# Operand halves loaded in place, ten gate tiles, and a reordered second projection in a hybrid decoder block

## The chip, the core and the metric

The kernel runs on one core of a Trainium2 chip. Its engines are TensorE (PE in the profile, with PEld for its weight loads), VectorE (DVE), ScalarE (ACT), GpSimd (POOL) and SyncE (SP, which issues nearly all transfers here). Each runs its own instructions in order and waits for the others by semaphores. The metric is device time in microseconds; smaller is better.

## The reference

One decoder block, batch 1, 1024 tokens of width 1024, all float32. Cut to the part in question:

```python
o_r = retention(qr, kr, vr)                         # 4 heads, chunks of 128 tokens, a running state
o_r = (head_groupnorm(o_r, ret_gn_g[l], ret_gn_b[l]) * jax.nn.silu(gr)).astype(x.dtype)
y = jax.nn.sigmoid(gate_a) * (o_a @ w_proj_a[l]) + jax.nn.sigmoid(gate_b) * (o_r @ w_proj_b[l])
x = x + y @ w_out[l]
```

Before it come an RMS norm, one input projection and dilated attention (whose result is o_a, 512 wide); behind it a squared-ReLU MLP.

## The kernel before

**Numbers in two halves.** A float32 operand x is used as a pair: xh, x rounded to the type that TensorE multiplies, and xl = x - xh. `split` (L349) makes the pair, xh on ACT (L350) and xl on DVE (L353). A product takes three matmuls a term: high by high, high by low, low by high. A group of 4 terms is 12 matmuls of 128x512.

**Stages around the change.** (1) *Retention*: 4 heads by 8 chunks of 128 tokens. For each chunk `values` multiplies the input by the head's value weights, and beside it run `decay`, `output`, `update` and, a chunk later, `turn_o`. `output` ends in a chain: ACT copies the result out of PSUM into `on` (L994), DVE takes its mean and variance (L996, L997, L998), POOL a power (L999), DVE scales (L1000, L1001). `turn_o` transposes `on` on TensorE (L1026, into `tr`), ACT scales it (L1031), and sums of it are stored to `on_d`, the operands of the second projection. (2) *First projection*: 16 groups (8 blocks of 128 outputs by 2 halves of the tokens), `oa` times w_proj_a; each result is multiplied with its gate (L1103 sigmoid on ACT, L1104 product on DVE) and stored to `pa_d`. (3) *Second projection*, tag "pb": 8 units j of 7 Strassen products, N1 to N7, each of one weight piece (A holds N1 and N2, B N6 and N3, C N5 and N7, D N4) with one operand of `on_d`. Units 0 to 3 take the first token half's operands, 4 to 7 the second's. `product` (L400) runs one and copies it out of PSUM (`ms` L419, `u` L424 and L427); `result` combines, gates and stores or, from unit 4 on, splits into the operands of (4) by `keep`. (4) *Output projection*, `w_out`.

**Where operands lie.** XS holds the block's input in three slots, (0,0), (1,0), (1,1), and a fourth, (0,1), while the retention needs them; ES are four slots that come free when the retention's tiles do. A slot is a pair xh, xl of 128 x 4 x 512. Before the change, `oa` (4 parts, `load_oa`) and the second projection's first operands are loaded into staging tiles of a pool of three (`pr`, name `oraw`, 512 KB each, `load_sum`) and split from there (`part_sum`); the later ones into tiles `s` of 256 KB (`load_part`), two splits for each 512 KB. The gates for (2) are loaded into a pool of four tiles (`pm2`) and, while ES[3] is unused, into its eight half rows (`places`, `spare`); a gate that lies there is written by its sigmoid into a tile of `pm2`.

**What sets the order.** TensorE's order is written out (L299, `manual_schedule`). A scheduler orders the other engines by its own estimate of times, but for instructions that `keep_in_program_order` pins to the place where the program calls them. Weights come by `Weights`: raw tiles are loaded in order as their places come free, and a list of steps splits them (and forms sums of them for B and C, `sums`). With `pace` 1 each `tick`, one a product, runs at most one step, no sooner than `lag` ticks behind the load of its raw tile. In the second projection `lag` is 2.

## Time and profile before

| | |
|---|---|
| median of 3 runs | 2179.03 us (2178.85 to 2179.24) |
| the profiled execution | 2176.74 us, its span 2175.0 us |
| TensorE idle in the span | 2175.0 - 2151.6 = 23.4 us |

By stretch, with the busy time of each engine (PE, PEld, DVE, ACT, POOL, each with the number of its instructions), the granted clock as a share of full speed, the DMA engines' busy share and GB/s:

```profile
1180.00:1285.00 105.00, 104.50 (x494) 85.64 (x493) 75.21 (x145) 59.13 (x116) 27.89 (x33) 1.00 0.56 168
1285.00:1320.00 35.00, 32.18 (x140) 25.67 (x138) 27.80 (x36) 22.15 (x31) 0.00 (x0) 1.00 0.93 318
1320.00:1400.00 80.00, 79.47 (x348) 64.90 (x347) 59.04 (x83) 41.49 (x68) 0.00 (x0) 1.00 0.77 263
1400.00:1470.00 70.00, 66.80 (x291) 54.03 (x290) 58.78 (x85) 35.60 (x54) 0.00 (x0) 1.00 0.75 243
```

The last head's end and the first projection lie in the first two rows, the second projection in 1300 to 1464. In a row of the timeline the first number is the start, the second the length; a bracket gives the idle time of that engine just before and what ended it. A row of a DMA is its issue; when it landed is another view.

### The profile page before, as it was taken

Reading aid. Unit: us, or ns where it says so; the run is one execution under the profiler, and the core shown is the slowest. Engines: PE = TensorE matmul, PEld = TensorE weight load, DVE = VectorE, ACT = ScalarE, POOL = GpSimd, SP = SyncE. Lnnn points to the kernel's source line nnn. Section 1 sums busy time; section 2 is a strip of 40 time slices with the busy share of each in tenths; the row PEclk is TensorE's granted clock in tenths of the full one; section 3 lists DMA queues with packets and bytes.
Section 4 is the critical chain, followed back from the end, with each engine's and each line's share of the span. In section 5 each row is a group of like instructions: output and inputs, shape, how many; then the busy total and the mean of one; then the engine's idle time right before and its main releaser. Section 6 shows DMA issues by size and latency. Waiting matters only on the chain. (4 is left out here: it accounts for less than half of the span.)

```text
span 2175.0 us, 28668 instructions
## 1 busy us (share of the span) xinstructions
PE 2151.6 (99%) x9928; PEld 1764.2 (81%) x9928; DVE 1356.0 (62%) x2327; ACT 1098.4 (51%) x2097; POOL 316.0 (15%) x340
## 2 busy tenths in 40 slices
PE   9999999999999999999999999999999999999999
PEld 6887777788888888888888877778788888888887
DVE  5723443565556665657776767783865556788884
ACT  5425555444655554545555655552654545755552
POOL 1000000000000000002123120000000000777773
PEclk9999999999999999999999999999999999999999
DMA  6323333333658676664364487774255556745443
GB/s 210 133 82 93 109 104 102 100 130 120 202 170 241 199 222 191 199 200 140 110 193 121 128 288 268 259 239 154 88 150 160 151 146 204 235 152 191 166 140 107
DMA packets 294579, 358.81 MB, mean 165 GB/s; under 512 B 35025, under 2 KB 202385, under 8 KB 294178
## 3 DMA queue, kind: packets, MB, share of 16 engines
q1 hardware_dynamic: 293890, 356.72, 52.4%
q8 instruction: 78, 1.28, 0.2%
q14 instruction: 67, 0.55, 0.1%
q10 hardware_dynamic: 544, 0.26, 0.0%
HBM read 240.33 MB, written 116.59 MB: 164 GB/s over the span
## 5 line engine op out<-in xcount | busy, mean ns | idle before, releaser
L353 DVE TENSOR_TENSOR wl<-raw,wh 128x1024 fp32r<-128x1024 f32 (+1 forms) x308 | 343.0, 1115 | 462.6 <-ACT wh L350 461.5
L350 ACT ACTIVATE wh<-raw 128x1024 fp32r<-128x1024 f32 (+1 forms) x308 | 296.0, 963 | 297.9 <-PE ms L247 106.6
L247 PE MATMUL mm<-xh,wh 128*128 128x512 f32 x960 | 387.7, 404 | 2.3 <-ACT ms L419 2.2
L247 PE MATMUL mm<-xl,wh 128*128 128x512 f32 x960 | 374.2, 390 | 0.9 <-DVE xl L353 0.9
L247 PE MATMUL mm<-xh,wl 128*128 128x512 f32 x960 | 375.0, 391 | 0.0
L247 PE MATMUL ms<-xh,wh 128*128 128x512 f32 x784 | 318.0, 406 | 4.5 <-ACT u L427 2.9
L247 PE MATMUL ms<-xh,wl 128*128 128x512 f32 x784 | 306.2, 391 | 1.4 <-DVE wl L353 1.4
L247 PE MATMUL ms<-xl,wh 128*128 128x512 f32 x784 | 305.6, 390 | 0.0
L247 PEld LDWEIGHTS mm<-xh,wl 128*128 128x128 f32 x960 | 180.2, 188 | 39.6 <-DVE wl L353 0.7
L247 PEld LDWEIGHTS mm<-xh,wh 128*128 128x128 f32 x960 | 180.5, 188 | 37.4 <-ACT ms L419 3.0
L247 PEld LDWEIGHTS mm<-xl,wh 128*128 128x128 f32 x960 | 180.7, 188 | 35.3 <-DVE xl L353 1.3
L247 PE MATMUL mm<-wh,xh 128*128 128x512 f32 x458 | 186.1, 406 | 0.1
L247 PEld LDWEIGHTS ms<-xh,wh 128*128 128x128 f32 x784 | 147.4, 188 | 45.2 <-issue 10.1
L999 POOL TENSOR_TENSOR st<-st,half 128x1 f32<-128x1 f32 x32 | 25.8, 807 | 1075.6 <-DVE st L998 1075.6
L247 PE MATMUL mm<-wh,xl 128*128 128x512 f32 x458 | 179.6, 392 | 0.9 <-DVE xl L353 0.9
L247 PE MATMUL mm<-wl,xh 128*128 128x512 f32 x458 | 178.5, 390 | 0.0
L247 PEld LDWEIGHTS ms<-xh,wl 128*128 128x128 f32 x784 | 147.1, 188 | 33.7 <-DVE wl L353 1.8
L247 PEld LDWEIGHTS ms<-xl,wh 128*128 128x128 f32 x784 | 147.6, 188 | 26.9
L247 PEld LDWEIGHTS mm<-wh,xl 128*128 128x128 f32 x458 | 86.0, 188 | 20.6 <-DVE xl L353 1.4
L247 PEld LDWEIGHTS mm<-wh,xh 128*128 128x128 f32 x458 | 86.2, 188 | 16.1 <-ACT xh L350 0.6
L247 PEld LDWEIGHTS mm<-wl,xh 128*128 128x128 f32 x458 | 86.5, 189 | 15.7
L247 PE MATMUL ms<-wh,xh 128*128 128x512 f32 x232 | 92.3, 398 | 0.0
(309 smaller groups left out, 3827.9 us busy)
## 6 DMA issues: line engine op xcount, KB each, us to landing
raw<-in_w_up SPq DMA_DIRECT2D x32, 512.0 KB, 3.8
h_d<-s SPq DMA_DIRECT2D x64, 256.0 KB, 4.3
raw<-in_w_down SPq DMA_DIRECT2D x32, 512.0 KB, 3.5
raw<-in_w_aqk_q SPq DMA_DIRECT2D x24, 512.0 KB, 3.5
qk_d<-sg SPq DMA_DIRECT2D x48, 256.0 KB, 3.0
qk<-qk_d SPq DMA_DIRECT2D x24, 512.0 KB, 5.8
rb<-rs_d SPq DMA_DIRECT2D x24, 512.0 KB, 7.1
xh<-h_d SPq DMA_DIRECT2D x11, 896.0 KB, 4.6
```

The lines of the kernel that those rows point to most:

```text
L247: self.nc.tensor.matmul(ps, x, y, start=start, stop=stop, skip_group_check=not first)
L350: hi = nc.scalar.activation(dst_h, src, AF.Copy)
L353: nc.vector.tensor_tensor(dst_l, src, dst_h.bitcast(F), op=OP.subtract)
L999: nc.gpsimd.tensor_tensor(st[:, 9:10], st[:, 8:9], half[:, 0:1], op=OP.pow)
```

## The change

**In-place landing.** `load_oa`, and `load_half` for all the second projection's operands, load 512 KB straight into the low half xl of the slot that they are for. The split then reads xl: ACT writes xh from xl, DVE writes xl from xl and xh (`split_halves`, pinned on ACT). The pool `pr`, `load_sum`, `part_sum` and `load_part` go. A load is issued a product at a time, its split follows three products later. Such a load has to wait until TensorE has read what lay in that half: `oa` comes into XS(0,0) and XS(1,0), which `values` reads up to chunk 3 of the last head, N5 and N7 into XS(0,1) and XS(1,1), which it reads up to chunk 7.

**Ten gate tiles.** `pm2` has ten tiles for four, `places` and `spare` go, a sigmoid is always in place, and up to two gates a step are loaded while fewer than eight are ahead.

**Second projection.** From unit 2 on the high part of each weight split is pinned, and the four sums are two steps of two instead of riding on D's step; `lag` is 3; the tick comes after the product's results and not before.

**Its end.** `keep` of the second token half of units 6 and 7, and the whole last result (that of N3 of unit 7), are put off until all products are issued (`last`); the result before it (N4 of unit 7) is pinned on DVE, with its split, and the splits of the first four blocks of `w_out` are pinned.

On TensorE and POOL the order of instructions is the same before and after. On ACT, DVE and SP it differs, at four places as follows.

*ACT, chunks 2 and 3 of the last head* (xh<-oraw, now xh<-xl, is a part of `oa`). Before:

```order
L350 ACTIVATE xh<-oraw 128x1024
L1031 ACTIVATE onE<-tr,gng 128x128 x4
L350 ACTIVATE xh<-oraw 128x1024
L350 ACTIVATE qh<-rqT 128x256
L994 ACTIVATE on<-ms 128x512
L350 ACTIVATE Sh<-St 128x512
L350 ACTIVATE xh<-oraw 128x1024
```

Now:

```order
L1044 ACTIVATE onE<-tr,gng 128x128 x4
L356 ACTIVATE xh<-xl 128x1024
L1007 ACTIVATE on<-ms 128x512
L356 ACTIVATE qh<-rqT 128x256
L356 ACTIVATE xh<-xl 128x1024
L356 ACTIVATE Sh<-St 128x512 x2
```

The split of a part of `oa` stands ahead of `on` in both, now directly ahead of it; and its transfer can now only leave when TensorE has read the low half. On DVE its xl stands ahead of BN_STATS in both.

*DVE, chunk 6 of the last head* (xl<-oraw,xh, now xl<-xl,xh, is a half of N5). Before:

```order
L353 TENSOR_TENSOR xl<-oraw,xh 128x1024
L996 BN_STATS st<-on 128x6
L1013 SCALAR_TENSOR_TENSOR St<-St,ms 128x512
L997 BN_AGGR st<-st 128x2
L1013 SCALAR_TENSOR_TENSOR St<-St,ms 128x512
L998 TENSOR_SCALAR st<-st,rc 128x1
L353 TENSOR_TENSOR Sl<-St,Sh 128x512
L1000 TENSOR_SCALAR st<-st,rc 128x1
L968 TENSOR_TENSOR sm<-ms,maskT 128x128
L1001 TENSOR_SCALAR on<-on,st 128x512
```

Now:

```order
L359 TENSOR_TENSOR xl<-xl,xh 128x1024
L1009 BN_STATS st<-on 128x6
L1026 SCALAR_TENSOR_TENSOR St<-St,ms 128x512
L1010 BN_AGGR st<-st 128x2
L1026 SCALAR_TENSOR_TENSOR St<-St,ms 128x512
L1011 TENSOR_SCALAR st<-st,rc 128x1
L359 TENSOR_TENSOR xl<-xl,xh 128x1024
L1013 TENSOR_SCALAR st<-st,rc 128x1
L359 TENSOR_TENSOR Sl<-St,Sh 128x512
L1014 TENSOR_SCALAR on<-on,st 128x512
L359 TENSOR_TENSOR Sl<-St,Sh 128x512
```

The split of N5's first half stands ahead of the chain from BN_STATS to `on` (L1001, now L1014) in both; that of its second half and one of the state's splits (Sl) now stand inside the chain.

*ACT in unit 1 to 3 of the second projection.* Before, with u the copies out of PSUM and wh the weight splits:

```order
L419 ACTIVATE ms<-mm 128x512
L350 ACTIVATE wh_11986<-raw_11915 128x1024
L909 ACTIVATE s<-s 128x512
L350 ACTIVATE wh_11961<-raw_11524 128x1024
L427 ACTIVATE u_11944<-ms 128x512
L909 ACTIVATE s<-s 128x512
```

Now:

```order
L427 ACTIVATE ms<-mm 128x512
L356 ACTIVATE wh_11919<-raw_11512 128x1024
L435 ACTIVATE u_11914<-ms 128x512
L910 ACTIVATE s<-s 128x512
L356 ACTIVATE wh_11944<-raw_11870 128x1024
L910 ACTIVATE s<-s 128x512
```

The copy `u` of L427 (now L435) stood behind two splits of 128x1024, and now stands behind one.

*DVE at the end of the second projection* (mm and u are the last products, wl are `w_out`'s splits, xl<-s,xh the operands of the output projection). Before:

```order
L1176 TENSOR_TENSOR s<-s,ms 128x512
L353 TENSOR_TENSOR wl_13092<-raw_12998,wh_13091 128x1024
L1177 TENSOR_TENSOR s<-s 128x512
L433 TENSOR_TENSOR u_12949<-mm,u_12949 128x512
L1178 TENSOR_TENSOR s<-s 128x512
L1180 TENSOR_TENSOR s<-s,u_12949 128x512
L353 TENSOR_TENSOR wl_13103<-raw_13043,wh_13102 128x1024
L353 TENSOR_TENSOR xl<-s,xh 128x512
L1181 TENSOR_TENSOR s<-s 128x512
L353 TENSOR_TENSOR xl<-s,xh 128x512
```

Now:

```order
L1181 TENSOR_TENSOR s<-s,ms 128x512
L1188 TENSOR_TENSOR s<-s 128x512
L1181 TENSOR_TENSOR s<-s 128x512
L359 TENSOR_TENSOR wl_12974<-raw_12883,wh_12973 128x1024
L1181 TENSOR_TENSOR s<-s 128x512
L441 TENSOR_TENSOR u_12847<-mm,u_12847 128x512
L359 TENSOR_TENSOR wl_12993<-raw_12927,wh_12992 128x1024
L359 TENSOR_TENSOR xl<-s,xh 128x512 x3
L1187 TENSOR_TENSOR s<-s,u_12847 128x512
L1188 TENSOR_TENSOR s<-s 128x512
L359 TENSOR_TENSOR xl<-s,xh 128x512
```

The three operations of one result (before L1176 to L1178, now L1181 three times) now all stand ahead of the last u, and of the last result's operations (before L1180 and L1181, now L1187 and L1188) those that stood ahead of the first xl now stand behind it.

The diff, cut to its core:

```diff
@@ -111,16 +111,18 @@
-                self.split(h, l, self.raw[r][:, cols], key[0] == "up" and key[1] < 2 and key[2] != "A")
+                late = key[0] == "pb" and key[1] > 1
+                self.split(h, l, self.raw[r][:, cols], late or key[0] == "up" and key[1] < 2 and key[2] != "A")
...
-        def sums(r):
+        def sums(r, which=(0, 1, 2, 3)):
             (x22, x21), (x11, x12) = ((self.raw[i][:, 0:512], self.raw[i][:, 512:1024]) for i in (r, r - 1))
-            for x, y in ((x22, x21), (x21, x11), (x11, x22), (x12, x11)):
+            for k in which:
+                x, y = ((x22, x21), (x21, x11), (x11, x22), (x12, x11))[k]
@@ -131,7 +133,10 @@
-                piece((tag, j, "D"), (self.D, j % 2), r, slice(0, 512), lambda r=r: sums(r))
+                fine = tag == "pb" and j > 1
+                piece((tag, j, "D"), (self.D, j % 2), r, slice(0, 512), None if fine else lambda r=r: sums(r))
+                if fine:
+                    self.steps += [(set(), r, lambda r=r, k=k: sums(r, k)) for k in ((0, 1), (2, 3))]
@@ -346,11 +352,13 @@
-    def split(dst_h, dst_l, src, pin=False):
+    def split(dst_h, dst_l, src, pin=False, both=False):
...
-        nc.vector.tensor_tensor(dst_l, src, dst_h.bitcast(F), op=OP.subtract)
+        lo = nc.vector.tensor_tensor(dst_l, src, dst_h.bitcast(F), op=OP.subtract)
+        if both:
+            tc.keep_in_program_order(lo)
@@ -898,19 +906,24 @@
-    def load_sum(from_, c, name, h):
-        raw = from_.tile([P, 2, 512], F, name="oraw")
-        o = 2 * SUMS.index(name)
-        nc.sync.dma_start(raw, on_d[2 * c + h, o:o + 2].rearrange("k p t -> p k t"))
-        return raw
...
-    def part_sum(to, raw, h):
-        split(*(x[:, 2 * h:2 * h + 2] for x in to), raw, True)
+    OPB = [{"N5": XS[0, 1], "N7": XS[1, 1]}, {}]
+    begun = []
+    def load_half(at, c, name, h):
+        xh, xl = (x[:, 2 * h:2 * h + 2] for x in OPB[c][name])
+        o = 2 * SUMS.index(name)
+        nc.sync.dma_start(xl.bitcast(F), on_d[2 * c + h, o:o + 2].rearrange("k p t -> p k t"))
+        begun.append((at, xh, xl))
+    def split_halves(upto):
+        while begun and begun[0][0] <= upto:
+            _, xh, xl = begun.pop(0)
+            split(xh, xl, xl.bitcast(F), True)
@@ -941,7 +954,7 @@
-            raw = pr.tile([P, S], F, name="oraw")
+            raw = oaS[s][1].bitcast(F)
@@ -1057,8 +1070,7 @@
-                    pr = pool(load, "pr", 3)
-                    pm2 = pool(load, "pm2", 4)
+                    pm2 = pool(load, "pm2", 10)
@@ -1072,35 +1084,28 @@
-                    raws = [(name, g, load_sum(pr, 0, name, g), -3) for name, g in (("N5", 0), ("N5", 1), ("N7", 0))]
+                    for name, g in (("N5", 0), ("N5", 1), ("N7", 0)):
+                        load_half(-3, 0, name, g)
...
-        OPB = [{"N5": XS[0, 1], "N7": XS[1, 1]}, {}]
         waiting = [("N7", 1)] + [(name, h) for name in ("N1", "N2", "N4", "N6") for h in range(2)]
-        spare = []
...
-            if len(gates) == n + 3 and n + 3 < len(work):
-                e, es = work[n + 3]
+            while len(gates) < min(n + 8, len(work)):
+                e, es = work[len(gates)]
                 gates.append(loaded(pm2, sg_d[0, e, :, es], "s0"))
-            for _ in range(2 if len(gates) < n + 8 else 0):
-                if spare:
-                    e, es = work[len(gates)]
-                    gates.append(spare.pop(0))
-                    nc.sync.dma_start(gates[-1], sg_d[0, e, :, es])
+                if len(gates) > n + 5:
+                    break
...
-                s0 = gates[n + 1]
-                if s0 in places:
-                    gates[n + 1] = pm2.tile([P, 512], F, name="s0")
-                tc.keep_in_program_order(nc.scalar.activation(gates[n + 1], s0, AF.Sigmoid))
+                sigmoid(gates[n + 1])
@@ -1109,19 +1114,12 @@
-                places = [x[:, k].bitcast(F) for x in ES[3] for k in range(4)]
-                spare = list(places)
...
-            if raws and raws[0][0] in OPB[0] and raws[0][3] <= n - 2:
-                name, h, raw, _ = raws.pop(0)
-                part_sum(OPB[0][name], raw, h)
-            if waiting and waiting[0][0] in OPB[0] and (n % 2 or n > 11) and len(raws) < 3:
-                name, h = waiting.pop(0)
-                raws.append((name, h, load_sum(pr, 0, name, h), n))
-        for name, h, raw, _ in raws:
-            part_sum(OPB[0][name], raw, h)
+            split_halves(n - 3)
+            if waiting and waiting[0][0] in OPB[0] and (n % 2 or n > 11):
+                load_half(n, 0, *waiting.pop(0))
@@ -1153,10 +1151,12 @@
-        def keep(j, f, cs, y):
+        last, done = [], []
+        def keep(j, f, cs, y, pin=False):
...
-            split(yh, yl, y)
+            split(yh, yl, y, pin, pin)
@@ -1171,16 +1171,25 @@
+            if n == len(results) - 1 and n in ahead and not done:
+                done.append(n)
+                last.append(lambda: result(j, f, cs, src))
+                return
...
-                nc.vector.tensor_tensor(y, y, src, op=OP.add)
-                nc.vector.tensor_tensor(y, y, sgb, op=OP.mult)
-                nc.vector.tensor_tensor(y, y, pa[0], op=OP.add)
+                for with_, op in ((src, OP.add), (sgb, OP.mult), (pa[0], OP.add)):
+                    ins = nc.vector.tensor_tensor(y, y, with_, op=op)
+                    if n == len(results) - 2:
+                        tc.keep_in_program_order(ins)
+                if n == len(results) - 2:
+                    return keep(j, f, cs, y, True)
...
+            elif j > 5 and cs.start and n < len(results) - 1:
+                last.append(lambda: keep(j, f, cs, y))
@@ -1189,26 +1198,21 @@
-        todo, unit = [(c, name, k) for c, name in ((0, "N3"),) for k in range(4)], {}
-        begun = []
-        def load_part(c, name, k):
-            return loaded(pm3, on_d[2 * c + k // 2, 2 * SUMS.index(name) + k % 2], "s")
+        todo, unit, base = [(0, "N3", h) for h in range(2)], {}, len(work)
+        W.lag = 3
...
-            todo += [(1, after[j, name], k) for k in range(4) if (j, name) in after]
+            pipe.tick()
+            todo += [(1, after[j, name], h) for h in range(2) if (j, name) in after]
             if (j, name) == (1, "N6"):
-                todo += [(1, "N1", k) for k in range(4)]
-            while begun and begun[0][0] <= i - 3:
-                _, c, op, k, raw = begun.pop(0)
-                split(*(x[:, k] for x in OPB[c][op]), raw)
-            while todo and len(begun) < 6 and (len(begun) < 2 or begun[-2][0] < i):
-                begun.append((i, *todo[0], load_part(*todo.pop(0))))
+                todo += [(1, "N1", h) for h in range(2)]
+            split_halves(base + i - 3)
+            if todo:
+                load_half(base + i, *todo.pop(0))
@@ -1219,6 +1223,8 @@
+        for fn in last:
+            fn()
```

13 lines of the change are left out of this document (7 added, 6 removed).

## The prediction

> **What bounds the kernel now.** I read the page's busy times first, then the waits of TensorE in the stretch that the change touches (1180 to 1480 us: the last retention head, the first projection, the second, the start of the output projection), then the timeline around each wait.
>
> ```profile
> PE 2151.6 (99%) x9928; PEld 1764.2 (81%) x9928; DVE 1356.0 (62%) x2327; ACT 1098.4 (51%) x2097; POOL 316.0 (15%) x340
> ```
>
> TensorE is busy 2151.6 of 2175.0 us, and the change leaves its instructions and their order alone. Only its waits can go or come. Those of 1180 to 1480 us, by who was waited for (total, times, longest):
>
> ```profile
> PE ms L247 <- DVE s L1104: 1.5, 2, 1.2
> PE ms L247 <- DVE wl L353: 1.4, 1, 1.4
> PE mm L247 <- ACT ms L419: 1.4, 1, 1.4
> PE ms L247 <- ACT u L427: 1.1, 2, 0.7
> PE mm L247 <- DVE xl L353: 0.9, 1, 0.9
> PE ms L247 <- ACT on L994: 0.3, 1, 0.3
> ```
>
> The first five are 6.3 us in seven waits. A matmul behind a wait lasts 0.50 us (1287.08 below) where its neighbours last 0.39 (1198.35 below), so I put each wait 0.13 us above its idle time: about 7.2 us, 0.33% of the span, is all that can be won there. The sixth lies in the retention, where the change adds waits of its own.
>
> **What the change can win, part by part.** *Ten gate tiles.* The wait for L1104 is a gate's product behind a late sigmoid:
>
> ```profile
> 1285.68 0.63 ACT L1103 ACTIVATE s<-xh 128x512 f32<-128x512 f32 x1 [2.69 <-DMA pa_d<-s]
> ...
> 1287.08 0.50 PE L247 MATMUL ms<-xh,wh 128*128 128x512 f32 x1 [1.23 <-DVE s L1104]
> ```
>
> ACT sat 2.69 us because, with four tiles, the next comes free only when a store to pa_d has landed. With ten, the first ten gates load during the retention, and the eleventh needs only the first's store. The idle 1.5 with two restarts is 1.7 us; I take all of it, and 1.0 as the low end, should one late store remain.
>
> *N6's halves.* The first N2 of the second projection waits for L419, which stands on ACT behind both splits of N6:
>
> ```profile
> 1306.69 1.06 ACT L350 ACTIVATE xh<-oraw 128x1024 fp32r<-128x1024 f32 x1 [0.25 <-DMA oraw<-on_d]
> 1307.66 0.58 ACT L419 ACTIVATE ms<-mm 128x512 f32<-128x512 f32 x1
> ...
> 1308.29 0.50 PE L247 MATMUL mm<-xh,wh 128*128 128x512 f32 x1 [1.35 <-ACT ms L419]
> ```
>
> The second split waited for its transfer. The two loads went out together; now the first stands one store earlier on SP and the second has its way alone. The least that this gives is the 0.25 of the row, the most the whole wait, 1.5; I take 1.2, since both splits can then run as soon as ACT is free.
>
> *Finer steps, lag 3, pinned splits.* An evacuation of u stands on ACT behind a weight split that waits for its transfer:
>
> ```profile
> 1324.99 1.06 ACT L350 ACTIVATE wh<-raw 128x1024 fp32r<-128x1024 f32 x1 [4.89 <-DMA raw<-in_w_pb_q]
> ```
>
> ACT stood still 4.89 us with u queued behind. Pinned and a product later, this split comes behind u in the order of ACT (third excerpt above). Both such waits, 1.1 and two restarts, are 1.4; I take all of it, 0.7 as the low end. For unit 7 the sums of the raw weights now stand in one run on DVE, and its split follows at once:
>
> ```profile
> 1436.45 0.69 DVE L124 TENSOR_TENSOR raw<-raw 128x512 f32<-128x512 f32 x1
> ...
> 1439.40 2.36 DVE L353 TENSOR_TENSOR wl<-raw,wh 128x1024 fp32r<-128x1024 f32 x2
> ...
> 1440.67 0.50 PE L247 MATMUL ms<-xh,wl 128*128 128x512 f32 x1 [1.42 <-DVE wl L353]
> ```
>
> From the last sum's end to that split lie 2.26 us of other DVE work, now behind it; but lag 3 lets the sums begin a product later, behind splits of their own. Of the 1.55 I take 0.9 (0 to 1.55).
>
> *The end.* The output projection's first tile waits for a split at the end of a DVE queue:
>
> ```profile
> 1464.28 1.23 DVE L353 TENSOR_TENSOR wl<-raw,wh 128x1024 fp32r<-128x1024 f32 x1
> 1465.41 0.69 DVE L353 TENSOR_TENSOR xl<-s,xh 128x512 fp32r<-128x512 f32 x1
> ...
> 1466.16 0.50 PE L247 MATMUL mm<-wh,xl 128*128 128x512 f32 x1 [0.94 <-DVE xl L353]
> ```
>
> Of what stands on DVE between the last product's u and this split, two operations of the kind of 0.69 us leave (last excerpt above; the row of 1465.41 has that length): up to 1.4 us against a wait of 0.94, so I take 1.0 (0 to 1.05). The results put off are first read by the output projection's last tiles of the same half; 24 matmuls of 0.23 us a tile cover them, and without that cover they would cost their 0.69 each.
>
> Gains: 1.7 + 1.2 + 1.4 + 0.9 + 1.0 = 6.2 us; the ends add to 2.0 and 7.2. The larger splits cost nothing: one of 1.22 on DVE for two of 0.69, on engines that are busy 62% and 51%.
>
> **What the change adds: loads that wait for TensorE.** A staged load could start whenever staging was free. One that lands in the operand's half waits for TensorE's last read of what lay there. Its split is pinned ahead of `on` on ACT (first excerpt above), so the price is set by L, the time from issue to landing of 512 KB. The retention's rows of 1100 to 1260 us, then those of the staged tile in the whole stretch:
>
> ```profile
> oraw<-on_d SPq DMA_DIRECT2D x6, 512.0 KB, 4.0
> ```
>
> ```profile
> L350 ACT ACTIVATE xh<-oraw x16: 1040/1053/1069, 1198.7 to 1306.7; 128x1024 fp32r<-128x1024 f32 x16
> L353 DVE TENSOR_TENSOR xl<-oraw,xh x16: 1217/1223/1810, 1199.8 to 1308.1; 128x1024 fp32r<-128x1024 f32 x16
> ...
> DMA to landing us min/median/max: 3.7/5.0/6.0
> ```
>
> Place 1, chunks 3 and 4 of the last head. What matters is the chain `on`, BN_STATS, ..., `on` (L1001), transpose:
>
> ```profile
> 1198.35 0.39 PE L247 MATMUL mm<-wh,xl 128*128 128x512 f32 x1
> ...
> 1203.62 0.69 DVE L996 BATCH_NORM_STATS2 st<-on 128x6 f32<-128x512 f32 x1
> ...
> 1207.03 0.55 DVE L1001 TENSOR_SCALAR on<-on,st 128x512 f32<-128x512 f32 x1
> 1207.05 0.40 PE L247 MATMUL mm<-wh,xl 128*128 128x512 f32 x1
> 1208.67 0.60 PE L1026 MATMUL tr<-ident,on 128*128 128x128 f32 x4
> 1209.57 1.28 ACT L909 ACT_TABLE_LOAD   x1
> ...
> 1213.87 0.69 DVE L996 BATCH_NORM_STATS2 st<-on 128x6 f32<-128x512 f32 x1
> 1217.76 0.54 DVE L1001 TENSOR_SCALAR on<-on,st 128x512 f32<-128x512 f32 x1
> 1218.77 0.60 PE L1026 MATMUL tr<-ident,on 128*128 128x128 f32 x4
> ```
>
> The first oa load leaves at 1198.74, when that read ends. Its xl split stands ahead of BN_STATS on DVE; from BN_STATS to the end of L1001 are 3.96 us. With 0.2 for hand-overs `on` is ready at 1198.74 + L + 1.05 + 1.22 + 3.96 + 0.2 = 1205.2 + L, and the transposes want it at 1208.67: a wait of L - 3.5. The last oa load leaves at 1207.45; behind its xh come the table load 1.28, a sigmoid 0.63, `on` 0.60, then 4.43 to the end of L1001: 1215.7 + L against 1218.77, L - 3.0. A first wait moves the second need along with it, so both together cost the larger: L - 3.0.
>
> Place 2, chunk 6, with N5's two halves:
>
> ```profile
> 1238.72 0.39 PE L247 MATMUL mm<-wh,xl 128*128 128x512 f32 x1
> ...
> 1244.93 0.68 DVE L996 BATCH_NORM_STATS2 st<-on 128x6 f32<-128x512 f32 x1
> ...
> 1248.14 0.45 SPq L905 DMA_DIRECT2D oraw<-on_d  x1
> 1248.42 0.54 DVE L1001 TENSOR_SCALAR on<-on,st 128x512 f32<-128x512 f32 x1
> ```
>
> The load leaves at 1239.11; BN_STATS starts at 1239.11 + L + 1.05 + 1.22 + 0.2 = 1241.6 + L. To L1001's end it is 4.03 now, and 0.85 more with the second xl of N5 and a split of the state now in between (second excerpt; 1.91, of which POOL's power hides about 1.05). That is 1246.5 + L against 1248.96 now, where there is no slack left (the transposes follow at once): L - 2.5.
>
> Place 3, N7's first half:
>
> ```profile
> 1253.54 0.60 ACT L994 ACTIVATE on<-ms 128x512 f32<-128x512 f32 x1
> 1254.20 0.50 PE L247 MATMUL ms<-vh,kzh 128*128 128x512 f32 x1 [0.32 <-ACT on L994]
> ```
>
> Its load still leaves at about 1248.14, behind three stores on SP. On ACT now follow xh 1.05, smh 0.3, four onT 1.5, `on` 0.60: it ends at 1251.8 + L, and TensorE, by then L - 2.5 later, wants it at 1251.3 + L: 0.5, of which 0.3 is there already. One gate product of 0.69 now stands between BN_STATS and the state's update, ahead of which it stood: 0.9 in all.
>
> New waits: (L - 3.0) + (L - 2.5) + 0.9 = 2L - 4.6, but not under 0. The rows' ends, 3.7 and 6.0, give 2.8 and 7.4; if the hand-overs and orders hide more than I see, 0. I take L = 4.0, the median of the six loads of this size in this stretch: 3.4 us.
>
> Two statements of the Trainium skill bear on L. "DMA: Bandwidth & Descriptors", on the anatomy of one DMA (the gpsimd path, whereas these go out from SP), fits a fixed 2.0 us plus the bytes over 436 GB/s, an estimate of 3.2 us for 512 KB; the measured 3.7 at least is slower, and by the page the new waits would be 1.8 and the time 1.6 us shorter than mine. "Perfetto Trace Analysis", DMA Optimizations, speaks against two per request: smaller transfers may let some work start sooner. In this trace 256 KB of the same data take 4.8 us (first row below) and 512 KB 5.0, so by the trace splitting would win back 0.2 of L, 0.4 us of the sum.
>
> ```profile
> s<-on_d SPq DMA_DIRECT2D x32, 256.0 KB, 4.8
> oraw<-on_d SPq DMA_DIRECT2D x12, 512.0 KB, 5.0
> ```
>
> **Sum.** 3.4 - 6.2 = -2.8 us. The profiled execution's 2176.74 (2175.0 and 1.7 around it) becomes 2173.9; the median shown, 2179.03, lies 2.3 above it, so the forecast is 2176.2 us.
>
> **Rivals.** *B: the new waits don't come.* For it: DMA is quiet in the retention, and two late loads may hide behind one another. Then the gains stand alone: 2179.0 - 6.2 = 2172.8, at most 2171.8. Against it: the orders put xh ahead of `on` in three chunks, and place 2 has no slack.
>
> *C: late landings make it slower.* One mechanism: in-place loads in the retention holding ACT, and behind it `on`. From L = 5.4 the new waits exceed 6.2 and the kernel is slower than before; at 6.0 with the gains at their low end of 2.0 it is 2179.0 + 7.4 - 2.0 = 2184.4. For it: a median of 5.0 and a maximum of 6.0 over the whole stretch; SP runs in order, so each load that waits for TensorE also holds the `sr`, `rqT` and weight loads behind it, which the formula leaves out. Against it: 4.0 in this part.
>
> *D: the gains only move.* DVE stays as full at the second projection's end as it was, ACT is held by another split; with gains of 3 and the new waits of 3.4: 2179.4. Against it: the orders show the late splits moved.
>
> **How the numbers follow.** Forecast 0.43, B 0.25, C 0.22, D 0.10. This kernel's measurement tells about 0.2% from no change: 2174.7 to 2183.4. Of the forecast's own spread (2173 to 2180, from L of 3.7 to 5.0 and the gains around 6) a third lies under 2174.7; B is faster; of C four fifths are slower, the rest within; D is within. Faster 0.15 + 0.25 = 0.40, slower 0.18, same 0.42. The range of 8 in 10 reaches from B's 2171.5 to C's 2183.5.
>
> **What would show it.** Right: no waits for a gate's product around 1285; L1001 and `on` late in chunks 3, 4 and 6 of the last head, with TensorE waiting at `tr` for some 1 us and 1.5 us; ACT idle before xh<-xl, ended by its DMA; waits for wl and xl at the second projection's end under 1 us. Wrong: no wait at `tr` there (B), or an issue-to-landing of xl<-oa_d and xl<-on_d above 5.4 (C), or a wait for u or ms as long as now (D).

## The result and the profile after

The changed kernel took 2185.11 us (median of 7 executions, 2183.78 to 2188.96) against 2178.85 of the kernel before, run between them (7, 2177.48 to 2180.46): ratio 1.0030, 95% interval 1.0020 to 1.0039. It is slower by 6.3 us; the forecast was 2176.2, and the range ended at 2183.5.

The profiled execution after has a span of 2187.2 us, 12.2 more than before. 3.3 of them lie ahead of the stretch that the change touches, 2.4 of these in the attention part (550 to 900 us). In the other profiled kernels that part ahead is between 0.6 us shorter and 4.2 us longer than before, so I don't put the 3.3 down to the change. In the stretch itself, 1180 to 1480 us, are 9.0, from the start of one matmul to the start of another, the same two in both. The profiled execution is the slowest of the seven, 3.9 us above their median. Busy times on the page after:

```profile
PE 2157.8 (99%) x9928; PEld 1769.3 (81%) x9928; DVE 1353.3 (62%) x2311; ACT 1094.9 (50%) x2081; POOL 315.0 (14%) x340
```

TensorE has the same 9928 matmuls and is busy 6.2 us longer: it doesn't only wait more, its work lasts longer too. The table of busy time by stretch (start:end, length, PE, PEld, DVE, ACT, POOL, then the granted TensorE clock, the DMA share and GB/s) shows where. Before:

```profile
1250.00:1300.00 50.00, 48.17 (x212) 38.34 (x211) 32.91 (x48) 26.05 (x44) 11.99 (x14) 1.00 0.87 290
1300.00:1350.00 50.00, 48.24 (x212) 39.26 (x211) 39.09 (x53) 28.65 (x43) 0.00 (x0) 1.00 0.79 263
1400.00:1450.00 50.00, 47.88 (x210) 38.98 (x209) 43.63 (x64) 27.00 (x42) 0.00 (x0) 1.00 0.80 268
```

After:

```profile
1250.00:1300.00 50.00, 46.82 (x203) 37.42 (x203) 32.00 (x53) 25.16 (x44) 14.39 (x17) 0.97 0.76 238
1300.00:1350.00 50.00, 47.82 (x204) 38.99 (x203) 34.48 (x44) 23.14 (x31) 0.00 (x0) 0.97 0.80 268
1400.00:1450.00 50.00, 46.67 (x193) 37.67 (x193) 42.69 (x60) 25.20 (x38) 0.00 (x0) 0.93 0.72 243
```

In 1400 to 1450 us 193 matmuls are done where 210 were, at a clock of 0.93 where it was 1.00. The waits of TensorE after, in 1180 to 1480 us (total, times, longest):

```profile
PE mm L252 <- ACT xh L356: 2.7, 1, 2.7
PE tr L1039 <- DVE on L1014: 2.5, 3, 1.1
PE mm L252 <- ACT ms L427: 2.2, 1, 2.2
PE ms L252 <- ACT on L1007: 1.3, 1, 1.3
PE ms L252 <- DVE s L1109: 0.8, 1, 0.8
PE mm L252 <- DVE xl L359: 0.7, 1, 0.7
PE ms L252 <- DVE wl L359: 0.5, 1, 0.5
```

With one of 0.2 for wh that is 10.9 us, where the six lines before add to 6.6. The old waits for a gate's product around 1285, both for u and that for xl at the end are gone, and unit 7's for wl is smaller. Three places are new or worse.

**The retention.** ACT's rows in chunks 3 and 4 of the last head, then TensorE's at the two transposes:

```profile
1205.71 1.06 ACT L356 ACTIVATE xh<-xl 128x1024 fp32r<-128x1024 f32 x1 [1.74 <-DMA xl<-oa_d]
1209.47 1.06 ACT L356 ACTIVATE xh<-xl 128x1024 fp32r<-128x1024 f32 x1 [1.91 <-DMA xl<-oa_d]
...
1213.01 0.66 PE L1039 MATMUL tr<-ident,on 128*128 128x128 f32 x4 [0.92 <-DVE on L1014]
...
1223.86 0.66 PE L1039 MATMUL tr<-ident,on 128*128 128x128 f32 x4 [0.52 <-DVE on L1014]
```

In chunk 3 it is not `on` itself that the second part holds. The state's high half Sh stands behind it on ACT, and DVE, inside the chain from BN_STATS to `on`, waits for Sh:

```profile
1211.08 0.69 DVE L359 TENSOR_TENSOR Sl<-St,Sh 128x512 fp32r<-128x512 f32 x1 [1.08 <-ACT Sh L356]
```

Chunks 6 and 7, ACT's splits of N5's first half and of N7's first:

```profile
1247.92 1.06 ACT L356 ACTIVATE xh<-xl 128x1024 fp32r<-128x1024 f32 x1 [0.55 <-DMA xl<-on_d]
...
1258.05 1.06 ACT L356 ACTIVATE xh<-xl 128x1024 fp32r<-128x1024 f32 x1 [2.56 <-DMA xl<-on_d]
```

```profile
1255.21 0.63 PE L1039 MATMUL tr<-ident,on 128*128 128x128 f32 x4 [1.10 <-DVE on L1014]
...
1261.23 0.50 PE L252 MATMUL ms<-vh,kzh 128*128 128x512 f32 x1 [1.25 <-ACT on L1007]
...
1263.01 0.50 PE L252 MATMUL ms<-xh,wh 128*128 128x512 f32 x1 [0.82 <-DVE s L1109]
```

ACT stands still until a half has landed, and TensorE waits for `on`, whose chain stands behind that half or has such splits in it. These are the prediction's places 1 to 3. In chunk 6 most of the wait is the chain's length: from the start of BN_STATS to the end of L1014 it takes 4.91 us, where it took 4.03, with the xl of N5's second half and one Sl now in it.

**The first N2 of the second projection.** Its wait grew from 1.35 to 2.18 us. ACT:

```profile
1315.08 1.06 ACT L356 ACTIVATE xh<-xl 128x1024 fp32r<-128x1024 f32 x1 [0.36 <-DMA xl<-on_d]
1316.05 1.06 ACT L427 ACTIVATE ms<-mm 128x512 f32<-128x512 f32 x2
```

The evacuation `ms` still stands behind N6's second split. By the semaphores in the trace that half left at 1307.62, just behind a half of N3 that is read later, and landed 7.4 us after its issue. Ahead of it ACT had stood still 2.40 us for N4's second half, whose split is pinned ahead of N6's. Transfers are slow in this stretch: from 1285 to 1320 us the DMA engines are busy 0.98 of the time, and its ten halves took 4.6 to 8.3 us (the view's last number is of the one load whose landing it tells):

```profile
xl<-on_d SPq DMA_DIRECT2D x10, 512.0 KB, 6.7
```

**Product 38,** the last product of the second operands' N3. Its half of N3 had landed at 1411.0, but its split stands on ACT behind the split of a result, which waited 4.87 us for DVE. ACT, then TensorE:

```profile
1417.98 0.63 ACT L356 ACTIVATE xh<-s 128x512 fp32r<-128x512 f32 x1 [4.87 <-DVE s L1181]
...
1419.47 1.04 ACT L356 ACTIVATE xh<-xl 128x1024 fp32r<-128x1024 f32 x1
```

```profile
1420.56 0.80 PE L252 MATMUL mm<-xh,wh 128*128 128x512 f32 x1 [2.68 <-ACT xh L356]
```

**Half rate behind the waits.** TensorE's rows around the N2 wait (start, duration):

```profile
1316.68 0.50 PE L252 MATMUL mm<-xh,wh 128*128 128x512 f32 x1 [2.18 <-ACT ms L427]
...
1318.26 0.63 PE L252 MATMUL mm<-xh,wh 128*128 128x512 f32 x1
```

From 1318.26 to 1321.25 seven matmuls start 0.43 us apart, elsewhere 0.227. The profile's record of the granted clock says half from 1318.06 to 1321.47, which begins 1.4 us after the wait's end. It happens three times, behind 1261 to 1263 (7 matmuls), behind 1316 (7) and behind 1420 (11): 25 x 0.20 = 5.0 us. The first two of these stretches, each with the one just ahead of it (the first number behind the length is PE's busy time, the third from the end the clock):

```profile
1260.03:1263.44 3.41, 1.39 (x5) 0.87 (x6) 3.41 (x8) 1.15 (x3) 1.51 (x3) 1.00 0.31 74
1263.45:1266.86 3.41, 3.41 (x10) 2.64 (x9) 2.43 (x7) 1.26 (x2) 1.83 (x3) 0.50 0.48 136
1314.65:1318.05 3.40, 1.37 (x6) 1.15 (x7) 3.40 (x5) 3.04 (x5) 0.00 (x0) 1.00 1.04 404
1318.06:1321.47 3.41, 3.41 (x10) 2.64 (x9) 3.38 (x4) 0.40 (x2) 0.00 (x0) 0.50 1.03 357
```

The third runs from 1420.46 to 1427.28, twice as long. The three begin 54.61 and 102.40 us apart, 16 and 30 times 3.413. In the 3.41 us ahead of them TensorE was idle 2.02, 2.04 and 2.58 us.

The Trainium skill describes this: "TensorE: Matmul & The Clock Gate", Part 1 (the HAM clock gate), has half clock after an idle window of some 3.4 us that runs freely, and its table on kernels asks for no idle gap above about 3 us. The 3.41 us of half rate and the spacing by whole multiples of it agree. The limit does not: here windows in which TensorE was idle for 2.0 of 3.4 us were enough, from one wait of 2.18 us, or from 1.25 and 0.82 close together.

### The profile page after: what moved, and what is told of

It reads as the page before. It is cut to its first block, busy times and chain, and to the rows that moved or that the text cites. A ratio compares the mean times of both kernels' runs of the same rounds, so it can differ in the third digit from the quotient of the medians.

```text
span 2187.2 us, 28561 instructions
## 1 busy us (share of the span) xinstructions
PE 2157.8 (99%) x9928; PEld 1769.3 (81%) x9928; DVE 1353.3 (62%) x2311; ACT 1094.9 (50%) x2081; POOL 315.0 (14%) x340
## 4 chain that ended last, share of the span: by engine, by line
PE 87%; DVE 5%; DMA 3%; ACT 2%; issue 2%; POOL 1%; SPq 0%; POOLq 0%; ACTq 0%; DVEq 0%
PE mm L252 44%; PE ms L252 37%; PE tr L671 1%; PE tr L692 1%; DVE xl L359 1%; DMA xl<-on_d 1%; ACT wh L356 1%; PE tr L682 1%; ACT xh L356 1%; PE tr L1039 1%; PE tr L824 1%; DVE raw L126 1%; PE ms L979 0%; DVE wl L359 0%; DMA raw<-in_w_rqk_q 0%
```

## The experiments

Waits below are TensorE's in 1180 to 1480 us of each kernel's profiled execution; "slow matmuls" are those at half rate there. The clock differs between executions of one kernel, so a profile and a median need not agree within 3 us. The kernel before ran beside each group of runs, with medians of 2177.7 to 2179.0 us; the ratios are to these.

| kernel | median us | ratio to before | waits us | slow matmuls |
|---|---|---|---|---|
| before | | | 6.6 | 0 |
| after | 2185.11 | 1.0030 [1.0020, 1.0039] | 10.9 | 25 |
| oa, N5, N7 staged again | 2186.57 | 1.0036 [1.0022, 1.0050] | 11.1 | 28 |
| N6 asked for earlier | 2186.66 | 1.0038 [1.0023, 1.0053] | 12.0 | 14 |
| N3's halves paired | 2181.76 | 1.0020 [1.0011, 1.0030] | 8.6 | 0 |
| third edit undone | 2184.22 | 1.0032 [1.0023, 1.0041] | 9.4 | 7 |
| late splits | 2180.48 | 1.0011 [1.0002, 1.0020] | 6.2 | 5 |
| late splits, pairs | 2174.92 | 0.9985 [0.9976, 0.9993] | 5.8 | 5 |
| and N6 earlier | 2177.14 | 0.9992 [0.9983, 1.0001] | 5.5 | 7 |
| before, end reordered alone | 2176.64 | 0.9986 [0.9978, 0.9995] | 5.2 | 0 |
| late splits, pairs, N6 ahead of N4 | 2177.26 | 0.9997 [0.9988, 1.0005] | 4.4 | 0 |
| same, finer sums for units 2 to 5 | 2174.86 | 0.9991 [0.9983, 1.0000] | 4.9 | 6 |
| same, old steps | 2173.77 | 0.9982 [0.9973, 0.9991] | 4.2 | 0 |
| same, old steps, all pins | 2174.52 | 0.9984 [0.9975, 0.9993] | 4.7 | 0 |
| same, old steps, pins of units 3 to 6 | 2170.43 | 0.9964 [0.9950, 0.9977] | 0.0 | 0 |

**The landing in the retention: staged again.**

```diff
-                    pm2 = pool(load, "pm2", 10)
+                    pr = pool(load, "pr", 2)
+                    pm2 = pool(load, "pm2", 6)
...
-            raw = oaS[s][1].bitcast(F)
+            raw = pr.tile([P, S], F, name="oraw")
```

> Edit of the changed kernel: oa and the first three halves (N5 twice, N7 once) are staged again, in a pool of two tiles, and the gates have six tiles. Theory A (the in-place loads of the retention make `on` late): the waits of TensorE for `tr` and `on` in the last head, 1.09, 0.69, 1.26, 1.41 and 0.99 us in the changed kernel, go back to under 0.6 us each, and the stretch of doubled matmul spacing behind them at 1263 to 1267 us (1.7 us lost) goes too: 5 to 7 us less than the changed kernel, 2178 to 2180 us. Rival B (they only move to the next wait): the two long waits of the second projection grow by as much, 2183 to 2186 us.

The waits in chunks 3, 4 and 6 went (0.3 lost is left at 1250), but that behind chunk 7 grew to 2.5 us, and the time is that of the changed kernel. With two staging tiles the third load (N7's first half) left at 1249.87, where with the three tiles of the kernel before it had left at 1211.91; in the changed kernel it waits for TensorE, here for a tile. So this run did not tell landing from place.

**N6 earlier, N3 paired.**

```diff
-            if waiting and waiting[0][0] in OPB[0] and (n % 2 or n > 11):
+            if waiting and waiting[0][0] in OPB[0] and (n % 2 or n > 9):
```

> Edit of the changed kernel: from the tenth group of the first projection on, not the twelfth, one operand half is loaded a step, so N6's second half leaves a step (2.7 us) earlier. Theory C (the wait of 2.2 us at the second projection's start is N6's late landing): that wait falls under 0.5 us, and the doubled spacing of the 8 matmuls behind it (1.6 us) goes: 3 to 4 us less, 2181 to 2182 us. Rival D (the DMA engines are full there, an earlier issue lands no earlier): the wait stays at 1.5 to 2.5 us and the time at 2184 to 2186 us.

The wait at the first N2 is 1.8 us and its drop of the clock stays: asking earlier in a stretch where the DMA share is 0.96 (1285 to 1320 us) brings little.

```diff
-            if todo:
-                load_half(base + i, *todo.pop(0))
+            for _ in range(2 if i > 28 else 1):
+                if todo:
+                    load_half(base + i, *todo.pop(0))
```

> Edit of the changed kernel: N3's and N4's halves of the second token half may leave two a product. Theory E (the wait of 2.7 us and its followers of 0.65 and 0.2 at unit 4's N3 come from a split queued on ACT behind a split of a result that DVE delivers late; a load one product earlier puts it ahead): the waits for ACT xh and DVE xl around 1420 us go, and with them the doubled spacing of 16 matmuls: 6 to 8 us less, 2177 to 2179 us. Rival F (DVE is simply full there): a wait of 2 us or more stays, for another tile, 2183 to 2186 us.

Product 38 now waits 0.8 us (for wl) instead of 2.7 and 0.7, no matmul is slow, and the median is 3.4 us lower (2.2 by the ratios, whose intervals overlap; in the profiles the stretch is 6.8 us shorter). Both splits of that N3 now run at 1409.5, ahead of the result's split that waits 4.86 us for DVE. In the kernel before the quarters came at the same rate, two a product, but their splits were not pinned; a pinned one stands where the program calls it, and the call came behind that result's.

**How long a wait halves the clock.** The kernel before with six waits of growing length in the up projection:

```diff
+            if name == "N5" and j in HOLD:
+                x = maskT[:, 0, :]
+                nc.vector.tensor_copy(x, unit[j]["d"][:, :P])
+                for _ in range(HOLD[j]):
+                    nc.gpsimd.tensor_tensor(x, x, maskT[:, 1, :], op=OP.add)
+                pt = tr.tile([P, 4, P], F, name="tr")
+                nc.tensor.transpose(pt[:, 0, :], x, ident)
```

> The kernel before with six waits of TensorE of rising length built into the MLP's first products (a copy on DVE, 1, 3, 4, 5, 6 and 8 operations on GpSimd, then a transpose that nothing reads), some 38 us apart. Theory G (a wait beyond some 2.3 us makes the matmuls behind it run at half the rate for some us): spacing stays at 0.227 us behind the short waits, and is about 0.43 us for 8 to 20 matmuls behind the waits over some 2.3 us, with the granted clock under 1.00 there. Rival H (the low clock is a state of the chip in those runs and no result of waits): the spacing is 0.227 us behind all six, and the time grows by the sum of the waits alone, some 14 us.

The waits lost 2.5, 3.0, 3.5, 4.1, 5.7 and 6.7 us, start to start. Behind the first two no matmul was slow, behind the others 6 to 9 each. Read alone this is a threshold between 3.0 and 3.5 us, and the 2.2 us of the changed kernel contradict it. Hence twelve waits of nearly one length (`HOLD = {j: 2 + j % 2 for j in range(2, 14)}`):

> The kernel before with twelve waits of TensorE put into the up projection, one per unit, made as before by a chain of POOL operations that a transpose waits for: three operations (about 3.0 us of wait) at odd units and two (about 2.7) at even ones. Matmuls at half rate behind a wait tell whether the clock dropped. If a fixed length of the wait decides (between 3.0 and 3.5 us, as the six waits before would have it), all twelve behave alike within each kind, and none drops. If the share of idle time in a window of the clock's own decides, then where the wait falls in that window matters: some of the twelve drop and others of the same length don't.

The 3.41 us ahead of and behind one boundary, for two of them (PE's busy time first, clock third from the end):

```profile
1615.79:1619.20 3.41, 1.47 (x7) 1.26 (x8) 1.04 (x3) 0.87 (x1) 1.28 (x2) 1.00 0.98 302
1619.21:1622.61 3.40, 3.40 (x10) 2.63 (x9) 1.23 (x1) 0.66 (x2) 0.00 (x0) 0.50 0.45 133
1639.68:1643.09 3.41, 1.50 (x7) 1.28 (x8) 0.67 (x2) 1.06 (x1) 1.70 (x3) 1.00 1.05 333
1643.10:1646.50 3.40, 3.40 (x16) 2.80 (x16) 1.04 (x1) 0.58 (x1) 0.00 (x0) 1.00 0.27 82
```

Seven waits cost 3.0 us and five 2.5. Ten of the twelve halved the clock, six of 3.0 us and four of 2.5; one of 3.0 and one of 2.5 did not. So the length alone does not decide. What decides can be read from the record of the clock. The ten stretches of half rate begin 7 or 13 times 3.413 us apart. Cut the run into windows of 3.413 us on that grid: TensorE was idle for 1.94 to 2.84 us in the window ahead of each of the ten. A boundary divided the other two waits, and their fuller windows had 1.91 and 1.89 us. Ten of the kept traces have such stretches. Over their windows at full clock, but for the first 30 us, 1.81 us is the least that drew one and 1.91 the most that did not, so the limit lies near 1.9 of 3.41 us. The first boundary lies anywhere from 0.4 to 3.0 us behind the start of these spans, whose first instructions are the same, so the program does not set the grid, and whether a wait of 2 to 3 us draws half rate is luck.

**Is it the landing, or the place of the split?** The in-place loads stay, their splits go to where the data are there:

```diff
-                if h == RH - 1 and c >= 4:
-                    load_oa(c - 4)
+                if h == RH - 1 and c == 4:
+                    sigmoid(gates[0])
+                    for s in range(SLOTS):
+                        load_oa(s)
+                for s in {5: (0, 1), 6: (2, 3)}.get(c, ()) if h == RH - 1 else ():
+                    split(*oaS[s], oaS[s][1].bitcast(F), True)
...
-                    for name, g in (("N5", 0), ("N5", 1), ("N7", 0)):
-                        load_half(-3, 0, name, g)
+                    for at, name, g in ((0, "N5", 0), (1, "N5", 1), (2, "N7", 0)):
+                        load_half(at, 0, name, g)
```

> The changed kernel with the retention's in-place loads kept at their places (oa's four now all asked for in chunk 4, N5's halves and N7's first half in the last chunk as before), but their splits put off to where their data have surely landed: oa's at the ends of chunks 5 and 6, N5's and N7's behind the gate products 3 to 5. Theory A (the waits that are new in the retention come from the place of the pinned splits on ACT and DVE, ahead of `on`): the waits of TensorE at the transposes behind chunks 3, 4 and 6 (1.1 + 0.7, 1.3, 1.4 + 1.0 us) sink under 0.5 us together or to what the kernel before has there (about 0.5), and so does the clock's drop behind the last of them (about 1.7 us): 5 to 6 us less than the changed kernel, about 2179.5. Theory L (it is the landing itself: the transfers wait for TensorE's last read and hold SP's queue): the waits stay within 1 us of the changed kernel's, and the time at 2184 to 2186. The waits in the second projection (2.3 and 2.8 us with their clock drops) are untouched in both.

Its waits in 1180 to 1480 us:

```profile
PE mm L252 <- ACT xh L356: 2.6, 1, 2.6
PE mm L252 <- ACT ms L427: 1.7, 1, 1.7
PE mm L252 <- DVE xl L359: 0.9, 1, 0.9
PE ms L252 <- DVE wl L359: 0.5, 1, 0.5
PE ms L252 <- DVE s L1111: 0.3, 1, 0.3
```

No wait for `on` is left, at `tr` or at `ms`; the median is 4.6 us under the changed kernel's (4.1 by the ratios), and in the profiles the stretch is 9.3 us shorter. The four loads of `oa` leave from 1200.93 to 1209.68, about where they left in the changed kernel (1202.02 to 1210.78). So landing in place costs TensorE nothing here; the pinned splits ahead of `on` and inside its chain did. With N3 in pairs as well:

> The same late splits, and the second operands N3 loaded two halves per product, so that their splits no longer come late at product 38. If stalls and the clock's drops behind them add up as theories A and E have it: 5 to 6 us (retention) and 3.4 us (product 38) less than the changed kernel, about 2176. Theory D (gains only move): the time saved shows as new waits elsewhere, and it stays over 2180.

2174.92, below the kernel before. The wait at the first N2 is now the longest (3.1 us). With N6 asked for earlier too:

> The kernel with late splits and paired N3 halves, and N6's halves asked for two gate products earlier (n>9 for n>11), so that an evacuation of the second projection stands ahead of N6's second split on ACT. If the wait at the second projection's first N2 (2.3 us and a clock drop of 1.6 in the changed kernel) is set by that order: it falls under 0.8 us, the granted clock stays 1.0 through 1180 to 1480 us, and the time is 2173 to 2176, below the kernel before. Theory D: that wait stays near 2 us, as it did when the halves were asked for earlier alone, and the time is 2176 to 2179.

Still 2.9 us there: it missed, as it had alone.

**The end alone, and the steps undone alone.** The end's edit put into the kernel before:

> The kernel before with only the end's reordering (the results that nothing waits for put behind the last product, the last but one pinned, w_out's first splits pinned). By the prediction's term: the wait of 0.94 at the output projection's first tile goes, 1.0 us less (0 to 1.05): 2177 to 2179, not to be told from the kernel before. If the results that are put off come too late for the output projection's last tiles, a wait of 0.7 or more stands there and nothing is gained.

2.4 us faster (interval 1.1 to 4.8), more than expected. In its profile both old waits of the end are gone, the 0.94 for xl and the 1.42 for unit 7's wl. The third edit undone in the changed kernel:

```diff
-                late = key[0] == "pb" and key[1] > 1
+                late = False
...
-                fine = tag == "pb" and j > 1
+                fine = False
...
-        W.lag = 3
```

The tick also goes back to the front of the product's results.

> The changed kernel with the second projection's steps as before the change (no late pinned splits, four sums in one step, no lag of 3): its third part undone alone, all else of the change kept. By the prediction's term (2.3 us won by this part) it is 2.3 us slower than the changed kernel, 2187. By the theory that this part only moved waits (as in the kernel with the new order of loads, where undoing it was 3.5 us faster): the waits of 0.4 and 0.7 us behind unit 7's split at the end and perhaps the one of 2.8 us at product 38 with its drop of the clock (the lag lets DVE's work pile up just ahead of it) go, some waits for u come: 2179 to 2182.

0.9 us faster by the medians, not by the ratios: no difference that can be told, where the prediction's term says 2.3 slower. Two waits for u came back (2.1 us together), those for wl and wh at the end went. The wait at product 38 stayed at 2.2 us: the finer steps had not made it.

**N6 ahead of N4, splits behind the evacuation.**

```diff
-        waiting = [("N7", 1)] + [(name, h) for name in ("N1", "N2", "N4", "N6") for h in range(2)]
+        waiting = [("N7", 1)] + [(name, h) for name in ("N1", "N2", "N6", "N4") for h in range(2)]
...
             product("pb", j, name, unit, OPB[j // 4], lambda: parts, result)
+            split_halves(base + i - 3)
             pipe.tick()
...
-            split_halves(base + i - 3)
```

> The kernel with late splits and paired N3 halves, with N6's halves fetched ahead of N4's (N6 is read by the fifth product of the second projection, N4 by the tenth), and the halves' splits issued right behind each product's own evacuation, so that the order of ACT is xh(N6), ms, xh(N4), ms, xh(N4), where it was xh, xh, ms, ms. Theory O (the wait at the second projection's first N2, 3.3 us with a drop of the clock in the kernel with late splits, comes from the evacuation standing behind a split whose half is late): the wait falls under 1 us, no drop of the clock in 1180 to 1480 us, some 4 us less than the 2174.9 of the kernel with late splits: 2170 to 2172. Theory D (transfers are the limit there, the share of DMA being 0.9; what is read next comes late instead): a wait of 2 us or more appears at the first N6 or N4, and the time stays at 2174 to 2176. The waits around 1415 and 1441 us (1.0; 1.1 and 0.7) are untouched.

The wait for `ms` is gone, so theory O holds for it; whether the order of the loads or the place of the splits did it, this run, which has both, doesn't tell. Others came:

```profile
PE mm L252 <- ACT wh L356: 1.4, 1, 1.4
PE ms L252 <- ACT wh L356: 1.2, 1, 1.2
PE mm L252 <- DVE wl L359: 1.1, 1, 1.1
```

Nothing was won in the median. The profiled execution took 2174.17 with a mean clock of 1.000; two others with 0.998 took 2179.14 and 2179.30. Three variants separate the parts of the third edit:

> The kernel just described with the second projection's steps as before the change (no late pinned splits, the four sums of the raw weights in one step, lag of one product less): the change's third part undone alone. The prediction gave that part 1.4 for two waits for u and 0.9 for unit 7's split, 2.3 us in all. If that holds, the two waits for u (about 0.75 each around 1365 and 1405 us) come back and unit 7's split waits longer than the 1.1 and 0.7 us that stand around 1441 us: 2 us slower. The rival: the end's reordering alone removed unit 7's wait (as in the kernel with that edit alone), and the finer steps put it back: then the waits of 1.1 and 0.7 go, those for u come, and the two kernels are within 0.5 us of one another.

> The kernel of the late splits and the new order with the late pinned splits kept and the finer steps only for units 2 to 5 (units 6 and 7 have their four sums in one step as before). If the waits of 1.0 around 1415 and of 1.1 and 0.7 around 1441 us come from the sums of units 6 and 7 cut into two steps, they go and the time falls by 2 to 3 us, to 2168 to 2170. If they come from the lag of 3 or the pins, they stay.

> The kernel of late splits, new order of loads and old steps (2173.8 us), with the late pinned weight splits put back alone: no lag of 3, no finer steps. If the pins are what helps the evacuations of u (the waits for u of 0.8 to 2.0 us there stand behind unpinned weight splits) and the lag of 3 is what hurts elsewhere (1314 and 1437 us): the waits for u go, none come for wh, 2169 to 2171. If the pins themselves make ACT late with wh: waits for wh of 1 us or more around 1314 and 1437, as with all of the new steps, and 2174 to 2178.

With the old steps it is 3.5 us faster, against the prediction's term, and by more than the rival's 0.5; its only waits:

```profile
PE ms L252 <- ACT u L435: 4.2, 4, 1.8
```

With the finer sums kept for units 2 to 5 the waits for wh and wl at 1316 and 1440 us stay. With the pins alone they are there too:

```profile
PE mm L252 <- ACT wh L356: 1.4, 1, 1.4
PE mm L252 <- DVE wl L359: 1.2, 1, 1.2
PE ms L252 <- ACT wh L356: 1.1, 1, 1.1
```

So it is the pins that make these waits: they trade the evacuations' waits for waits of the pinned splits' own, at unit 2's and unit 7's weights. The 3.5 us are not theirs: the pins alone are as fast as the old steps (0.9984 and 0.9982). With all the new steps 8 of 11 executions have a mean clock of 0.998 or 0.999, with the old ones none, so half rate may be where the 3.5 us lie; no profile shows it, since the profiled one with the new steps is among those at 1.000. The last run drops the two pins:

```diff
-                late = key[0] == "pb" and key[1] > 1
+                late = key[0] == "pb" and 2 < key[1] < 7
```

> The kernel of late splits, new order of loads and old steps with the late pinned weight splits for units 3 to 6 alone. With the pins for units 2 to 7 the waits for u (4.2 us in four) went, and waits for wh and wl came at 1315 (1.6 and 1.3, unit 2's weights) and 1438 us (1.3 and 0.7, unit 7's). If each pin sets only its own unit's wait, the waits at 1315 and 1438 go and most of those for u stay away: 2 us of waits where the others have 4 to 5, about 2172. If the waits only move between u and wh, 4 us of waits remain, and 2174.

Every wait in the stretch is gone; its table of stretches:

```profile
1300.00:1350.00 50.00, 50.00 (x222) 41.42 (x221) 37.27 (x46) 25.95 (x35) 0.00 (x0) 1.00 0.82 282
...
1400.00:1450.00 50.00, 50.00 (x222) 41.36 (x221) 46.42 (x67) 28.95 (x45) 0.00 (x0) 1.00 0.79 252
```

2170.43 us (5 executions, 2169.18 to 2171.58) is 14.7 us under the changed kernel and 7.5 under the kernel before beside it (5.0 to 10.9), a little better than expected, since no wait is left. This version has the change's in-place landing, gate tiles and end, with the split places, load order and pins changed, the second operands' halves in pairs, and the old sums and lag.

## Why the prediction was wrong

Time lost from one matmul's start to the next, beyond 0.227 us, where TensorE waited or ran at half rate, by the prediction's terms, in the two profiled executions:

| term | predicted | before | after | change |
|---|---|---|---|---|
| waits for `on` in the retention | +3.4 | 1.0 | 5.4 | +4.4 |
| gates' products | -1.7 | 1.8 | 0.2 | -1.6 |
| first N2 (N6's halves) | -1.2 | 1.5 | 2.3 | +0.8 |
| waits for u | -1.4 | 1.7 | 0.0 | -1.7 |
| unit 7's split | -0.9 | 1.6 | 1.1 | -0.5 |
| the end | -1.0 | 1.4 | 0.0 | -1.4 |
| product 38 | none | 0.0 | 4.4 | +4.4 |
| half rate, 25 matmuls | none | 0.0 | 5.0 | +5.0 |
| sum | -2.8 | | | +9.4 |

The stretch grew by 9.0 us, so the rows account for it to within 0.4. The rows leave out that the matmul behind a wait lasts longer, 0.11 us each.

**The retention: right in mechanism, too low in size.** The places and the chain (transfer, xh on ACT, `on`, transpose) held, with L from 3.6 to 5.6 us for the eight loads. Place 1 was priced L - 3.0 for both its waits. The last part of `oa` took 4.6 us by the trace's semaphores, which gives 1.6, and 0.92 + 0.52 was measured; that Sh would stand behind the second part was not seen. Place 2 was priced L - 2.5. N5's first half on SP:

```profile
1244.29 0.36 SPq L919 DMA_DIRECT2D xl<-on_d  x1
```

From here to its split (1247.92) are 3.6 us. With these for L that is 1.1, and 1.10 was measured. Place 3 was too low: 0.9 was said, of which 0.3 was there already, and 1.25 and 0.82 came. In "Its load still leaves at about 1248.14" the "still" was misread: by the semaphores N7's first half had left at 1211.91 in the kernel before, and the load at 1248.14 is another half's. That the time nearly held is luck. The load left at 1253.88, with TensorE 5.1 us late by then, so 0.6 later than the sum has it, and took 4.1 us where N5's first half took 3.6; the sum had one L for both. The estimate of 3.2 us for L from the fit of the Trainium skill ("DMA: Bandwidth & Descriptors", anatomy of one DMA) was below every L measured here.

**The gates and the end: right.** The gates' term was read only in traces: the waits for gate products are 0.3 with ten tiles (late splits) and 2.3 with four (the end alone). The end is worth 2.4 us by its own run. The 0.9 that I had given to the finer sums was the end's: with its edit alone unit 7's wait went.

**N6's halves: wrong.** The step "both splits can then run as soon as ACT is free" failed, and with it "the second has its way alone": the second half left 0.6 us behind a half of N3 and took 7.4 us, and ACT stood still for N4's second half before it. As long as the evacuation stands behind such splits, it is late by whichever lands last. Asking earlier did not help, while a new order with the splits behind the evacuation did.

**Finer steps: right in sight, wrong in sum.** The waits for u went as said. Rival D had it that "ACT is held by another split", and that is what the pins at unit 2 and unit 7 do; 0.10 was too little for it. Undoing the whole third edit costs nothing in the changed kernel and wins 3.5 us in the median of the one with late splits and the new order.

**Product 38: a term put at nothing.** "The larger splits cost nothing", I wrote, from their own length and from engines that are busy 62% and 51%, and did not ask what the pinned ones stand behind. One result's split that waited 4.87 us for DVE reached TensorE through one of them: 4.4 us, of which 1.0 was left when the halves were loaded in pairs.

**The clock: the largest term, put at nothing.** "I put each wait 0.13 us above its idle time" left half rate out. The stretches of it behind 1.3 + 0.8, 2.2 and 2.7 + 0.7 us of waits cost 1.4, 1.4 and 2.2 us. The 0.13 was small even for the kernel before, which has no half rate in this stretch: the gate's product at 1287.08 waited 1.23 us, and the two starts behind it came 1.50 us late, 0.27 more. So the 7.2 us that "is all that can be won there" were too few: the rows of the kernel before add to 8.0 without the retention and to 9.0 with it, and the stretch of the last run, with no wait left, is 9.6 us shorter than before.

Without half rate the sum would be +4.4, with neither it nor product 38 zero, still 2.8 above what was forecast. So no one term made the sign. These 5.0 us are of the profiled execution, at a mean clock of 0.997; the fastest of the seven, at 0.999, took 2183.78 us and so was slower than the kernel before as well. Rival C's time (2184.4) came close by luck: its one mechanism, at an L of 6.0 in the retention, is not what the runs show.

## What to carry to other kernels

Where a transfer lands in place, put its split behind the point where it has surely landed, and behind the evacuations that the next product needs; a pin is worth it only for splits whose own consumer has slack. Add up TensorE's waits over any 3.4 us: where they reach about 1.9 us, allow for a stretch of half rate behind them, mostly 1.4 us more, which comes or not by where the clock's windows fall. When a change wins in one place and loses in another, undo its parts one by one: here the same parts in another order gave 2170.4 instead of 2185.1.

## What the runs showed of the hardware

The TensorE clock is granted at half for 3.41 or 6.83 us, on a grid of 3.413 us that the program does not set, when TensorE was idle for about 1.9 us or more of the window ahead (1.94 to 2.84 drew it, 1.89 and 1.91 did not, in the run of twelve waits; one case at 1.81 elsewhere). So waits of 2.5 and of 3.0 us halved it in ten of twelve cases. In 1180 to 1480 us it cost 5 to 11 matmuls of 512 columns 0.20 us each.

It goes with part of the spread between executions: with the finer sums for units 2 to 5, the three executions at a mean clock of 1.000 took 2171.78 to 2174.86 us and the three at 0.998 took 2178.88 to 2179.80. It is not all of it, since in one group of 21 executions the kernel before took 2175.60 to 2180.75 us, at 0.999 or 1.000 throughout.
